# Moving two norms, their PSUM banks and two weight buffers in a two-block layer on one core

## The chip, the cores and the metric

The kernel runs on one core of one Trainium2 chip. The metric is device time in microseconds; before the change the median of three runs is 2661.46 us (2647.43 to 2663.86).

## The reference, cut to what matters

Two transformer blocks follow each other on 1024 tokens of 1024 features. What the change touches is the place where each mixer hands over to its feed-forward part, and the place where the first feed-forward hands over to a gate.

```python
# first block
y = concat([rmsnorm(y_c, g_out_conv), rmsnorm(y_a, g_out_attn)])
x = x + y @ w_out
h = rmsnorm(x, g_ffn)
gate = causal_dwconv3(h @ w_gate, ffn_conv_w, ffn_conv_b)
x = x + (silu(gate) * (h @ w_up)) @ w_down          # D_FF = 2816
x = x + sigmoid(rmsnorm(x, g_ple) @ w_ple_gate) * (p @ w_ple_proj)
# second block
x = x + concat([out_a, out_b]) @ w_out_2
h2 = rmsnorm(x, norm2_w)
x = x + (silu(h2 @ w_gate_2) * (h2 @ w_up_2)) @ w_down_2
```

## The kernel before

Features lie on the partitions, tokens on the free axis, in tiles of 128 x 1024; the tokens are worked on in two halves of 512. A product of full precision is three matmuls (lines 99 to 101): weights and activations are split into a high and a low part (the copy of line 93 on ScalarE, the subtraction of line 94 on VectorE or GpSimd) and high x high, high x low, low x high are added up in one PSUM bank.

A norm (class `Norm`) gathers squares of each tile into `acc` (line 129 on ScalarE, line 130 on VectorE). `rstd` then needs two banks, which it takes from the ring that it is given: four matmuls with ones (line 142) put the sums into the first, VectorE scales them (line 108), GpSimd raises them to the power -1/2 (line 109), and four transposes (line 145) spread the result over the second bank, from which VectorE reads it while it scales the tiles (line 157 in `apply`, line 645 in `Operands`).

The up and gate products of the feed-forward (`Quads`) use seven products per 2 x 2 group of weight and token halves, named 1, 2, 6, 7, 5, 4, 3. The first four pairs of weight tiles (gate and up in turn) go together: products 1 and 2 of all four need only the first half of the tokens (`Operands.first`), so eight products are issued before the first that needs the second half (`Operands.second`: norm of the second half, eight scalings at line 645, twelve subtractions at lines 669 to 672, four splits, and the loads of each pair's other weight tile at line 712, into buffers that the scalings set free). Each product is twelve matmuls. The eight products use all eight banks, two a pair. Weights pass through a ring of eight split buffers. Products 1 and 2 are taken out of the banks at line 804 (ScalarE) and line 806 (VectorE).

`out_part` multiplies the normed attention with its half of `w_out`, eight groups of twelve matmuls for a half of the tokens, adds to the residual at line 616, stores it (line 618 on SP's queue) and feeds the norm. Its banks come from `c.ring`, all eight in order.

`Down` runs the down product in four stages of eleven steps, with its own ring of split buffers that includes the `whi` and `wlo` tiles. The last three steps of stage 3 are held back and run bank by bank. `s4` holds six tiles of weight sums for stage 3. After it, `ple` loads the gate's weights (line 83) into the two `c.wraw` tiles in turn, splits them into `whi` and `wlo` tiles and multiplies.

Buffers of 128 x 1024 are units of one list: `take` pops the one that was given back longest ago, `take_last` the newest; an instruction that writes a taken unit waits for the last users of that unit. The order of the instructions on each engine is worked out when the kernel is built, with the program's order as priority, so neighbouring steps interleave; it is fixed from then on.

Of the kernel before, what the change touches and what calls it, by code (L numbers as in the profile page):

```python
# [20 lines left out]
HALF = (slice(0, 512), slice(512, 1024))  # L21
# [82 lines left out]
def rsqrt(c, ss, n, scale, eps):  # L104

    nc = c.nc
    r = c.small.tile([128, 32], F32, name="rq")
    nc.vector.tensor_scalar(r[:, 0:n], ss, scale, eps, OP.mult, OP.add)  # L108
    nc.gpsimd.tensor_tensor(r[:, 16:16 + n], r[:, 0:n], c.mhalf[:, 0:n], OP.pow)  # L109
    return r[:, 16:16 + n]  # L110


class Norm:
# [20 lines left out]
    def rstd(self, hs, ring):  # L134

        c = self.c
        nc = c.nc
        p, b = ring(), ring()
        n = 4 * len(hs)
        for j in range(n):  # L140
            o = hs[j // 4] * 512 + j % 4 * 128
            nc.tensor.matmul(p[:, j:j + 1], self.acc[:, o:o + 128], c.ones, start=True, stop=True)
        r = rsqrt(c, p[:, 0:n], n, 1.0 / self.nfeat, self.eps)
        for j in range(n):
            nc.tensor.transpose((b, p)[j // 4][:, j % 4 * 128:j % 4 * 128 + 128],
                                r[:, j:j + 1].to_broadcast([128, 128]), c.ident)
        return (b, p)[:len(hs)]

    def last(self, ring):
        rb, = self.rstd((1,), ring)  # L150
        self.c.give(self.acc)
        return rb
# [17 lines left out]
def pairs(his, los):  # L170
    return [(a.bitcast(F32R), b.bitcast(F32R)) for a, b in zip(his, los)]
# [343 lines left out]
def mixer1(c, a, h, xs, proj, norm_x):  # L515

    acts = pairs(*h)
    ring = Cycle(c.bank[0:2])
    tabs = c.takes(2)
    c.tab = Cycle(tabs)  # L520
    c.q, c.k, c.v, c.ya = {}, {}, {}, {}
    c.yc = [c.dr.tile([128, 1024], F32, name=f"yc{j}") for j in range(4)]

    def fill():
        yield from first
        norm_c = Norm(c, 512, c.vec["g_out_conv"], 1e-6)
        cv = conv_branch(c, a, acts, ring, norm_c)
        g1 = qkv_group(c, a, 1, acts, ring)
        for g, n in ((cv, 12), (g1, 24), (cv, 12)):
            for _ in range(n):  # L530
                next(g)
                yield
        next(cv, None)
        c.give(*h)
        yield from out_conv(c, a, ring, xs, norm_c, at)
        while len(c.ya) < 4:
            yield
        ya.extend(c.ya[i] for i in range(4))
        hi.extend(c.takes(4))
        lo.extend(c.takes(4))  # L540
        at.norm.apply(ya, hi, lo, 0, ring)
        yield
        yield from out_part(c, a["w_out"][1], pairs(hi, lo), ring, xs, (0,), norm, ws=ws, store=c.xf)
        rb.extend(norm.rstd((0,), ring))

    norm, ws = Norm(c, D, c.vec["g_ffn"], 1e-6), {}
    ya, hi, lo, rb = [], [], [], []
    first = qkv_group(c, a, 0, acts, ring)
    for i in range(17):
        next(first)  # L550
        if i in (1, 3):
            next(norm_x)
        if i >= 1:
            next(proj, None)
    filler = fill()
    at = Attention1(c, a, ring)
    for _ in at.pack(0):
        next(filler)
    at.run(filler, (2.08, 2.2, 2.5, 2.68))
    c.give(tabs)  # L560
    for _ in filler:
        pass
    ops = Operands(c, 4)
    at.norm.apply(ya, hi, lo, 1, Cycle(c.bank[2:4]))
    c.give(ya)
    ops.first(norm, xs, rb[0])
    quads = Quads(c, ops, hidden_pairs(a["w_gate"], a["w_up"]))
    for _ in out_part(c, a["w_out"][1], pairs(hi, lo), c.ring, xs, (1,), norm, ws=ws, store=c.xf):
        pass
    c.give(hi, lo)  # L570
    return quads, norm.last


def out_conv(c, a, ring, xs, n, at):

    nc = c.nc
    hi, lo = [], []
    rb = n.rstd((0, 1), ring)
    c.give(n.acc)
    for j in range(4):  # L580
        yc, p, l = c.takes(3)
        hi.append(p)
        lo.append(l)
        nc.sync.dma_start(yc, c.yc[j])
        for h in range(2):
            n.one(yc, j, p, l, h, rb[h], nc.gpsimd if h else nc.vector)
        c.give(yc)
        if j % 2:
            yield
    at.sums()  # L590
    yield from out_part(c, a["w_out"][0], pairs(hi, lo), ring, xs, (0, 1), load=a["xT"])
    c.give(hi, lo)
# [97 lines left out]
class Quads:  # L690
# [42 lines left out]
    def run(self, jobs, rstd, last):  # L733

        c, g = self.c, self.GROUP
        self.prep(2 * g)
        late, banks = {2 * g + 1: 7, 3 * g: 5, 3 * g + 2: 4, 3 * g + 4: 3}, {}
        for i, (n, p) in enumerate(self.steps):  # L740
            if i == 2 * g:
                self.acts.second(rstd(Cycle([banks[0][1], banks[1][1]])),
                                 lambda j: self.load(j, 1, c.take_last()))
            if i >= 2 * g:
                self.prep(i + 8)
            if i in late:
                self.acts.rest(late[i])
            if n not in banks:
                banks[n] = c.ring(), c.ring()
            bank = banks[n][0 if p in (1, 6, 5, 3) else 1]  # L750
            self.product(p, bank, self.ops.pop(0))
            if n == len(jobs) - 1:
                c.give(self.acts.u.pop(p))
                last(p, self)
            jobs[n](p, bank)
# [125 lines left out]
class Down:  # L881
# [53 lines left out]
    def operands(self, stage, j):  # L935
        c = self.c
        tt = c.nc.vector.tensor_tensor
        x, v = self.x.pop((stage, j)), self.v.pop((stage, j), None)
        if stage == 0:
            return self.parts(self.kept[j]), self.parts(x)  # L940
        if stage == 1:
            if j % 2 == 0:
                self.s4.append(c.take())
            u, w = self.kept.pop(j), c.take()
            tt(w[:, LO], v[:, LO], v[:, HI], OP.add)
            tt(w[:, LO], w[:, LO], u[:, LO], OP.subtract)
            tt(w[:, HI], u[:, LO], v[:, LO], OP.subtract)
            tt(self.s4[j // 2][:, HALF[j % 2]], u[:, HI], w[:, LO], OP.subtract)
            r = self.parts(w), self.parts(x)
            c.give(w)  # L950
            if j < 4:
                self.xs[2 * j + 1] = self.dma(u, self.xd[2 * j + 1])
            else:
                c.give(u)
            return r
        if stage == 2:
            tt(v[:, LO], v[:, LO], v[:, HI], OP.add)
            return self.parts(v), self.parts(x)
        return self.parts(self.s4[j // 2][:, HALF[j % 2]]), self.parts(x)

    def product(self, j, i, m, p, ops):
        w, x = ops
# [24 lines left out]
    def run(self):  # L987
        c, n = self.c, self.N
        extra = self.ring.items[:4]
        for stage, ps in enumerate(STAGES):  # L990
            tail = []
            for j in range(n):
                at = stage * n + j
                self.load(at + 6)
                ops = self.operands(stage, j)
                if stage == 3 and j >= n - 3:
                    tail.append((j, ops))
                    continue
                for i, p in enumerate(ps):
                    for m in range(4):  # L1000
                        self.product(j, i, m, p, ops)
                if stage == 0 and j in (4, 5, 6, 7):
                    t = 2 * (j - 4)
                    self.xs[t] = c.take()
                    self.dma(self.xs[t][:, LO], self.xd[t][:, LO])
                elif stage == 2 and j in (4, 5, 6, 7):
                    t = 2 * (j - 4)
                    self.dma(self.xs[t][:, HI], self.xd[t][:, HI])
                elif stage == 3 and j == 3 and self.norm is not None:
                    xl = [self.xs[m] for m in range(8)]  # L1010
                    nh, nl = c.takes(8), c.takes(8)
                    self.norm.apply(xl, nh, nl, 0, Cycle(self.b))
            if stage < 3:
                self.sums(stage)
            else:
                for m in range(4):
                    for j, ops in tail:
                        self.product(j, 0, m, 3, ops)
                    self.add(2 * m, 1, self.a[m])
        c.give(extra, self.s4, self.ring_x.items)  # L1020
        c.wraw = c.takes(2)
        if self.norm is None:
            return None
        return xl, (nh, nl), lambda: self.norm.apply(xl, nh, nl, 1, Cycle(self.b))
# [875 lines left out]
```

## Time and profile before

| | |
|---|---|
| median of 3 runs | 2661.46 us (2647.43 to 2663.86) |
| the profiled execution, its own time | 2663.26 us |
| its span, first to last instruction | 2661.5 us |
| mean granted TensorE clock | 0.968 |
| PE, busy | 2549.1 us |
| VectorE / ScalarE / GpSimd, busy | 1722.6 / 1121.5 / 318.7 us |

Times in the rows are microseconds from the start of the span. A row of a timeline gives the start, the duration, the engine, the source line, the operation with its result and operands, how many were merged, and in brackets how long the engine had been idle before and whose work ended that. PE is matmul, DVE is VectorE, ACT is ScalarE, POOL is GpSimd, SPq is the queue on SP that issues the transfers. A clock of 1.00 is 2.4 GHz, one of 0.50 is 1.2 GHz. Work of line 142 and 145 is recorded with one or two records for each instruction.

### The profile page before, as it was taken

How to read it: one execution, taken by the hardware profiler on the slowest of the kernel's cores; microseconds unless marked ns; L12 is line 12 of the kernel's file. 1: busy time of each engine (PE TensorE's matmuls, PEld its weight loads, DVE VectorE, ACT ScalarE, POOL GpSimd, SP SyncE). 2: the span in 40 equal slices, each digit the busy share in tenths (PEclk: the TensorE clock that was granted, in tenths of full speed). 3: DMA queues.
4: the chain of work that ended last, by engine and by line, in shares of the span. 5: the costliest groups of instructions: out<-in, count | busy, mean ns of one | idle time of the engine just before them, and what ended most of it. 6: DMA issues, size and time to landing. Idle time of an engine off the chain costs nothing.

```text
span 2661.5 us, 35653 instructions
## 1 busy us (share of the span) xinstructions
PE 2549.1 (96%) x13706; PEld 2114.5 (79%) x13706; DVE 1722.6 (65%) x3020; ACT 1121.5 (42%) x1913; POOL 318.7 (12%) x299
## 2 busy tenths in 40 slices
PE   8999999977999999999899999989996999999999
PEld 7978877765888887888689989877775888888787
DVE  6443445446877776776666899695658665565854
ACT  5333434233544444334444656544554433333332
POOL 3101001020000000000342233352220000000000
PEclk9999999978999999999899999899997999999999
DMA  6111113011232325744352322331111332237643
GB/s 224 48 40 40 49 48 127 33 64 64 99 108 107 111 105 171 245 138 135 115 204 75 118 78 96 111 108 48 33 68 68 131 107 95 99 108 249 215 154 118
DMA packets 103322, 289.59 MB, mean 109 GB/s; under 512 B 11208, under 2 KB 20464, under 8 KB 103152
## 3 DMA queue, kind: packets, MB, share of 16 engines
q1 hardware_dynamic: 101360, 281.03, 30.9%
q0 software_dynamic: 1792, 6.29, 0.6%
q8 instruction: 107, 1.75, 0.3%
q14 instruction: 63, 0.52, 0.1%
HBM read 211.77 MB, written 75.51 MB: 108 GB/s over the span
## 4 chain that ended last, share of the span: by engine, by line
PE 81%; DVE 9%; DMA 3%; issue 3%; ACT 2%; POOL 1%; SPq 0%; POOLq 0%; DVEq 0%; ACTq 0%
PE m L99 19%; PE m L100 19%; PE m L101 19%; PE m L426 3%; PE m L276 3%; PE m L278 3%; PE m L277 3%; PE m L417 3%; DVE t L94 2%; PE m L398 2%; PE m L397 2%; DVE t L1173 1%; DMA t<-in_w_down_dram 1%; ACT t L93 1%; POOL t L94 1%
## 5 line engine op out<-in xcount | busy, mean ns | idle before, releaser
L99 PE MATMUL m<-t,t 128*128 128x512 f32 x2520 | 976.1, 398 | 61.9 <-ACT t L93 55.2
L100 PE MATMUL m<-t,t 128*128 128x512 f32 x2520 | 989.2, 393 | 2.9 <-DVE t L94 2.3
L101 PE MATMUL m<-t,t 128*128 128x512 f32 x2520 | 975.4, 393 | 1.1 <-DVE t L94 1.1
L93 ACT ACTIVATE t<-t 128x512 fp32r<-128x512 f32 (+1 forms) x706 | 520.4, 758 | 872.2 <-PE m L100 612.6
L94 DVE TENSOR_TENSOR t<-t,t 128x512 fp32r<-128x512 f32 (+1 forms) x650 | 571.3, 900 | 274.0 <-ACT t L93 260.0
L99 PEld LDWEIGHTS m<-t,t 128*128 128x128 f32 x2520 | 480.0, 191 | 172.9 <-ACT t L93 61.0
L100 PEld LDWEIGHTS m<-t,t 128*128 128x128 f32 x2520 | 478.0, 190 | 103.7 <-DVE t L94 4.1
L101 PEld LDWEIGHTS m<-t,t 128*128 128x128 f32 x2520 | 476.7, 189 | 103.9 <-DVE t L94 3.5
L276 PE MATMUL m<-t,t 128*128 128x256 f32 x896 | 263.2, 294 | 3.1 <-DVE t L1613 2.5
L278 PE MATMUL m<-t,t 128*128 128x256 f32 x896 | 258.5, 289 | 3.5 <-DVE t L94 2.8
L277 PE MATMUL m<-t,t 128*128 128x256 f32 x896 | 257.6, 288 | 0.0
L109 POOL TENSOR_TENSOR rq<-rq,mhalf 128x4 f32<-128x4 f32 (+1 forms) x56 | 80.1, 1432 | 1005.7 <-DVE rq L108 988.5
L276 PEld LDWEIGHTS m<-t,t 128*128 128x128 f32 x896 | 174.9, 195 | 9.2 <-DVE t L1613 3.1
L278 PEld LDWEIGHTS m<-t,t 128*128 128x128 f32 x896 | 174.9, 195 | 5.9 <-DVE t L94 3.2
L277 PEld LDWEIGHTS m<-t,t 128*128 128x128 f32 x896 | 175.0, 195 | 1.9 <-issue 1.4
L403 ACT ACTIVATE t<-t,ar 128x256 f32<-128x256 f32 (+7 forms) x128 | 98.9, 773 | 92.3 <-DVE ar L400 89.2
L426 PE MATMUL m<-t,t 128*64 128x128 f32 x1152 | 107.5, 290 | 1.3 <-ACT t L423 0.7
L1170 ACT ACTIVATE t<-t,yss 128x896 f32<-128x896 f32 (+2 forms) x96 | 86.1, 897 | 47.1 <-DVE yss L1183 37.4
L423 ACT ACTIVATE t<-m 128x512 f32<-128x512 f32 (+3 forms) x128 | 56.6, 461 | 108.4 <-PE m L417 108.1
L616 DVE TENSOR_TENSOR t<-m,t 128x512 f32<-128x512 f32 x72 | 49.3, 688 | 79.6 <-PE m L101 75.7
L426 PEld LDWEIGHTS m<-t,t 128*64 128x64 f32 x1152 | 74.9, 141 | 32.0 <-issue 22.3
L400 DVE CUSTOM_DVE_ANT_0 t<-m,t 128x512 f32<-128x512 f32 (+3 forms) x128 | 73.8, 586 | 40.9 <-PE m L398 16.0
(225 smaller groups left out, 2649.2 us busy)
## 6 DMA issues: line engine op xcount, KB each, us to landing
t<-hd SPq DMA_DIRECT2D x66, 512.0 KB, 3.6
t<-in_w_down_dram SPq DMA_DIRECT2D x66, 512.0 KB, 4.3
t<-in_w_gate_dram SPq DMA_DIRECT2D x48, 512.0 KB, 3.8
t<-in_w_up_dram SPq DMA_DIRECT2D x44, 512.0 KB, 3.7
hd<-t SPq DMA_DIRECT2D x44, 512.0 KB, 2.9
hd<-t SPq DMA_DIRECT2D x66, 256.0 KB, 2.5
t<-in_w_out_dram SPq DMA_DIRECT2D x16, 512.0 KB, 3.5
xf<-t SPq DMA_DIRECT2D x32, 256.0 KB, 2.0
```

The source lines that it names most:

```text
L93: self.nc.scalar.activation(hi.bitcast(F32R), x, AF.Copy)
L94: (eng or self.nc.vector).tensor_tensor(lo.bitcast(F32R), x, hi, OP.subtract)
L99: nc.tensor.matmul(out, w[0], a[0], start=first, stop=False, skip_group_check=skip)
L100: nc.tensor.matmul(out, w[0], a[1], start=False, stop=False, skip_group_check=skip)
L101: nc.tensor.matmul(out, w[1], a[0], start=False, stop=last, skip_group_check=skip)
L109: nc.gpsimd.tensor_tensor(r[:, 16:16 + n], r[:, 0:n], c.mhalf[:, 0:n], OP.pow)
L276: nc.tensor.matmul(out, ah, wk[0], start=k == 0, stop=False)
L277: nc.tensor.matmul(out, ah, wk[1], start=False, stop=False)
L278: nc.tensor.matmul(out, al, wk[0], start=False, stop=k == NK - 1)
L403: nc.scalar.activation(p[:, :n], p[:, :n], AF.Exp, bias=least, scale=-1.0, accum_out=c.den[:, j:j + 1])
L426: nc.tensor.matmul(o[r], self.v(2 * hp + e, kb), ps[e][:, kb * 128:(kb + 1) * 128], start=kb == 0, stop=kb == qi)
L1170: nc.scalar.activation(ja[:, :s.shape[1]], s, AF.Sign, bias=NV[:, j:j + 1], accum_out=ca[:, j:j + 1])
```

## The change

Three places are edited.

1. In the first block, the norm of the feed-forward's first half no longer gets its `rstd` at the end of the work that fills the attention, in banks 0 and 1. It gets it after the second half of the attention's own norm, and both use banks 2 and 3, in the same order.
2. In `Quads.run` (both blocks), `second` is issued after the first pair's two products instead of after all eight, and its `rstd` uses the two banks of the fourth pair instead of one each of the first and second. The banks of the four pairs are handed out ahead, in the order as before.
3. In `Down`, each `s4` tile is given back as soon as it has been split in stage 3, and with a norm to follow (first block) the two `wraw` tiles are taken in step 3 of stage 3, ahead of the sixteen tiles of the normed result, instead of at the end.

```diff
@@ mixer1
         at.norm.apply(ya, hi, lo, 0, ring)
         yield
         yield from out_part(c, a["w_out"][1], pairs(hi, lo), ring, xs, (0,), norm, ws=ws, store=c.xf)
-        rb.extend(norm.rstd((0,), ring))
...
     ops = Operands(c, 4)
-    at.norm.apply(ya, hi, lo, 1, Cycle(c.bank[2:4]))
+    two = Cycle(c.bank[2:4])
+    at.norm.apply(ya, hi, lo, 1, two)
     c.give(ya)
-    ops.first(norm, xs, rb[0])
+    ops.first(norm, xs, norm.rstd((0,), two)[0])
@@ Quads.run
         self.prep(2 * g)
         late, banks = {2 * g + 1: 7, 3 * g: 5, 3 * g + 2: 4, 3 * g + 4: 3}, {}
+        for n in range(g):
+            banks[n] = c.ring(), c.ring()
         for i, (n, p) in enumerate(self.steps):
-            if i == 2 * g:
-                self.acts.second(rstd(Cycle([banks[0][1], banks[1][1]])),
-                                 lambda j: self.load(j, 1, c.take_last()))
+            if i == 2:
+                self.acts.second(rstd(Cycle(banks[g - 1])), lambda j: self.load(j, 1, c.take_last()))
@@ Down.operands
-        return self.parts(self.s4[j // 2][:, HALF[j % 2]]), self.parts(x)
+        r = self.parts(self.s4[j // 2][:, HALF[j % 2]]), self.parts(x)
+        if j % 2 or j == self.N - 1:
+            c.give(self.s4[j // 2])
+        return r
@@ Down.run
                 elif stage == 3 and j == 3 and self.norm is not None:
+                    c.wraw = c.takes(2)
                     xl = [self.xs[m] for m in range(8)]
                     nh, nl = c.takes(8), c.takes(8)
...
-        c.give(extra, self.s4, self.ring_x.items)
-        c.wraw = c.takes(2)
+        c.give(extra, self.ring_x.items)
```

## Rows read from the trace of the kernel before

**Rows 1.** The page, section 1: busy us (share of span) x instructions

```profile
PE 2549.1 (96%) x13706; PEld 2114.5 (79%) x13706; DVE 1722.6 (65%) x3020; ACT 1121.5 (42%) x1913; POOL 318.7 (12%) x299
```

**Rows 2.** The waits of PE, whole span: waiter, releaser, us, times, longest

```profile
PE m L99 <- ACT t L93: 55.2, 10, 14.5
```

**Rows 3.** PE's timeline after the first attention: start, us, engine, line, count, idle before

```profile
578.45 1.71 PE L142 MATMUL m<-ones,t 128*128 128x1 f32 x8
...
589.89 1.11 PE L145 MATMUL m<-ident,rq 128*128 128x128 f32 x4 [9.73 <-POOL rq L109]
...
592.50 3.78 PE L99 MATMUL m<-t,t 128*128 128x512 f32 x8 [1.50 <-ACT t L93]
```

**Rows 4.** DVE's timeline there

```profile
577.15 0.69 DVE L130 TENSOR_TENSOR t<-t,t 128x512 f32<-128x512 f32 x1 [0.63 <-ACT t L129]
...
578.70 5.36 DVE L645 SCALAR_TENSOR_TENSOR t<-t,vecs,m 128x512 f32<-128x512 f32 x8 [0.86 <-PE m L145]
```

**Rows 5.** POOL's timeline there

```profile
580.25 8.62 POOL L94 TENSOR_TENSOR t<-t,t 128x512 fp32r<-128x512 f32 x7 [2.58 <-PE m L142]
...
588.83 1.00 POOL L109 TENSOR_TENSOR rq<-rq,mhalf 128x4 f32<-128x4 f32 x1
```

**Rows 6.** PE's timeline, first block, from eighth product to full rate

```profile
638.95 0.94 PE L142 MATMUL m<-ones,t 128*128 128x1 f32 x8
...
656.42 1.40 PE L99 MATMUL m<-t,t 128*128 128x512 f32 x2 [14.54 <-ACT t L93]
...
664.79 0.80 PE L101 MATMUL m<-t,t 128*128 128x512 f32 x1 [0.52 <-DVE t L94]
...
670.56 0.39 PE L99 MATMUL m<-t,t 128*128 128x512 f32 x1
```

**Rows 7.** DVE's timeline, first block, from end of sums to second norm

```profile
619.02 1.48 DVE L130 TENSOR_TENSOR t<-t,t 128x512 f32<-128x512 f32 x2
...
622.89 0.69 DVE L806 TENSOR_TENSOR t<-m,t 128x512 f32<-128x512 f32 x1 [2.39 <-PE m L101]
...
641.92 5.36 DVE L645 SCALAR_TENSOR_TENSOR t<-t,vecs,m 128x512 f32<-128x512 f32 x8 [1.83 <-PE m L145]
```

**Rows 8.** SP's queue there, first of four loads

```profile
643.40 0.33 SPq L712 DMA_DIRECT2D t<-in_w_gate_dram  x1
```

**Rows 9.** Windows, first block: us, busy by engine, granted clock, DMA

```profile
650.00:665.00 15.00, 4.59 (x8) 2.08 (x9) 15.00 (x26) 8.98 (x15) 0.00 (x0) 0.50 0.06 24
```

**Rows 10.** DVE's timeline, second block

```profile
1993.39 1.46 DVE L94 TENSOR_TENSOR t<-t,t 128x512 fp32r<-128x512 f32 x1
...
2005.97 3.79 DVE L130 TENSOR_TENSOR t<-t,t 128x512 f32<-128x512 f32 x5
...
2021.93 5.36 DVE L645 SCALAR_TENSOR_TENSOR t<-t,vecs,m 128x512 f32<-128x512 f32 x8 [1.61 <-PE m L145]
```

**Rows 11.** PE's timeline, end of first down product and start of gate

```profile
1264.13 0.95 PE L142 MATMUL m<-ones,t 128*128 128x1 f32 x8
...
1270.74 0.60 PE L145 MATMUL m<-ident,rq 128*128 128x128 f32 x4
...
1282.11 0.39 PE L101 MATMUL m<-t,t 128*128 128x512 f32 x1
...
1293.64 0.79 PE L99 MATMUL m<-t,t 128*128 128x512 f32 x1 [11.14 <-ACT t L93]
...
1298.06 0.44 PE L99 MATMUL m<-t,t 128*128 128x512 f32 x1
```

**Rows 12.** The waits of SP's queue there

```profile
SPq L83 <- DVE t L130: 8.8, 2, 8.3
```

**Rows 13.** ACT's timeline there

```profile
1288.01 0.63 ACT L129 ACTIVATE t<-t 128x512 f32<-128x512 f32 x1 [0.21 <-DVE t L130]
...
1292.54 1.06 ACT L93 ACTIVATE t<-t 128x1024 fp32r<-128x1024 f32 x1 [3.89 <-DMA t<-in_w_ple_gate_dram]
```

**Rows 14.** POOL's timeline, second block

```profile
1986.75 10.95 POOL L94 TENSOR_TENSOR t<-t,t 128x512 fp32r<-128x512 f32 x8 [1.30 <-ACT t L93]
```

More of the change, by code (lines that the diff above doesn't have):

```diff
@@ L543, in fill @@
         yield from out_part(c, a["w_out"][1], pairs(hi, lo), ring, xs, (0,), norm, ws=ws, store=c.xf)
-        rb.extend(norm.rstd((0,), ring))
     norm, ws = Norm(c, D, c.vec["g_ffn"], 1e-6), {}
-    ya, hi, lo, rb = [], [], [], []
+    ya, hi, lo = [], [], []
     first = qkv_group(c, a, 0, acts, ring)
```

## The prediction

> **What bounds the kernel now.** I read the page first: PE is busy for 96% of the span [rows 1], so only stretches in which PE waits, or runs slowly, can be won. Next the waits of PE: one kind stands out, the first matmul of a product waiting for ScalarE's split, 55.2 us in ten waits [rows 2]. PE's timeline shows where the long ones lie, and each is a place that the change edits.
>
> Place A, after the first attention. PE's in-order queue holds the transposes of the attention's second-half norm (line 145), and they start only at 589.89, after 9.73 us of waiting for the power on GpSimd [rows 3]. The sums they need were complete at 577.84, when VectorE ended line 130; but VectorE then did eight scalings of the other norm (578.70 to 584.06) [rows 4], and GpSimd did seven splits for them, 580.25 to 588.87, before it reached the power at 588.83 [rows 5]. The norm that PE needs stands behind work that PE needs 25 us later. The output product starts at 592.50.
>
> Place B, in both feed-forwards. PE ends the eighth product at 638.95, makes the sums of the second norm, and then starts product 6 at 656.42 after 14.54 us of idling; its third matmul kind comes at 664.79 and full rate at 670.56 [rows 6]. VectorE is what runs meanwhile: its scalings start at 641.92 [rows 7], the first of the four loads for these weights is issued at 643.40 [rows 8], and from 650 to 665 VectorE is busy 15.00 of 15.00 us with PE's clock granted at 0.50, the 1.2 GHz level, after that idling [rows 9]. The second block repeats it, with the scalings at 2021.93 [rows 10].
>
> Place C, the ple gate. PE ends the down product at 1282.5 and waits 11.14 us, until 1293.64 [rows 11]. The waits of SP's queue say why: line 83, the load of the gate's weights, waited up to 8.3 us for VectorE's line 130 [rows 12]. The two `wraw` units were the only free ones left, and the norm's last squares had used them.
>
> **Rates.** Product 2 is evacuated at 622.89 [rows 7] and product 8 ends at 638.95 [rows 6]: six products in 16.1 us, 2.68 us each or 0.223 us a matmul. So product 1 began near 617.5.
>
> **Part A.** One `rstd` moves behind the other: the same four sums, one scaling, one power, four transposes, no instruction added or removed. In before's rows the chain is 1.71 us for the sums at the slow clock and 2.61 us from the transposes' start to the first matmul [rows 3]; the power takes 1.00 us [rows 5], and some 0.6 us go for VectorE's step and hand-overs (my estimate, from the gaps of these rows). That is 5.9 us after 577.84, 583.8 instead of 592.50: 8.7 us won, 7 if PE also makes the other norm's sums first (1.7 us). I take 8.6. What is late next: the moved norm must wait for the four readers of bank 3, then its eight scalings (5.4 us), ScalarE and eight GpSimd splits, 1.23 us each, run beside the output product. Scalings from about 587 to 592 and splits until 600 end well before product 1, now at 608.9; that cover is about 8 us. `out_part`'s fourth group wants bank 3 as well, at about 594, 2 us behind the last scaling; if the transposes are issued 6 us late, PE loses up to 6 us there. VectorE has, beside it, the residual additions it had before.
>
> Here a rule of the chip speaks against the move. In the second block eight GpSimd splits already run beside the output product, 1986.75 to 1997.70 [rows 14], and VectorE's split took 1.46 us there [rows 10], where an operation of that shape alone takes 0.69 [rows 7]. In the first block five of VectorE's splits and accumulations would now lie beside them: 5 x 0.7 = 3.5 us, and the sums before place B, complete 2.2 us before product 2 ends [rows 7], would be at most 1.3 us late. The Trainium skill ("SBUF — State Buffer", section "SBUF: two separate sides") says that VectorE with two SBUF inputs and GpSimd lock the shared port pair for a whole instruction and the loser fully blocks. By that rule the five could each lose a whole GpSimd split of 1.23 us, 6 us in all, the sums would be about 4 us late and the forecast some 3 us higher; the row shows about half of that for one instruction.
>
> **Part B.** `second` is moved past six products: one `rstd`, eight scalings, twelve subtractions, four splits (24 on VectorE, about 0.6 us apart), four on ScalarE, and four loads on SP. The loads pass nothing that waits long: SP then holds only the residual's stores, whose additions end before. The earliest it can start is the later of the sums' end and product 2's end. Product 2 then ends at 608.9 + 5.4 = 614.3. From sums to scalings took 2.97 us in before (638.95 to 641.92) [rows 6, 7], when PE had nothing else to do. Where PE has, the build's order puts products between: 1264.13 to 1270.74, 6.6 us [rows 11], the shortest of three such pairs; then 0.7 us to the scalings. Between 617.3 and 621.6 I take 620.6, near the late end since the three pairs resemble the new place.
>
> From there VectorE's chain sets product 6, in before and after alike. In before PE did 21 matmuls (4.7 us) from 638.95 to full rate at 670.56, so its steady run began in effect at 665.9, 24.0 us after the scalings. The same chain after 620.6, and two or three evacuations of line 806 that fall into it (1.5 us), gives 646.1. Won in the first block, A and B together: 665.9 - 646.1 = 19.8 us, of which B is 11.2. Ends: 23.1 (transposes at once) plus 2.6 if the clock does not fall, and 13 with the losses named under A. The bank costs nothing: the fourth pair's second product comes at about 629, the scalings have left its bank by 626.
>
> In the second block the sums are late: VectorE runs five accumulations of line 130 in a row from 2005.97, ending at 2009.76 [rows 10], while product 2 ends near 2002.9 (2.97 us and six products before 2021.93). So PE's queue may meet the sums a few us early and stall; that is hidden, as PE would idle before product 6 anyway. Scalings then start between 2012.7 and 2017.1, against 2021.93; less 1.8 us of evacuations inside the chain this wins 7.4 to 3.1 us. I take 5.
>
> **Part C.** Two oldest units instead of the last two: nothing wrote them since stage 1 or so, so the loads can go when SP has issued the inputs of stage 3; ScalarE waited 3.89 us for one that it had nothing else to do beside [rows 13], so one issued by 1278 costs nothing. The early return of `s4` makes up for the two units, and costs nothing itself. What is late next is the split buffer: `whi` and `wlo` are used by the last held-back steps, so ScalarE's split (1.06 us [rows 13]) can start only at PE's end, 1282.5, and PE at 1284.0 if ScalarE is free. If the build puts the norm's squares first, which end at 1288.64 [rows 13], PE starts at 1289.7. In before the loss was 13.6 us: full rate came at 1298.06 after nine matmuls (2.0 us) [rows 11]. In after it is 1.5 to 3 us, or at the other end 9.2 with 2 us of slow clock. Won: 12 to 4.4; I take 9, nearer to the early end, since the split needs only PE's end, the squares also an addition after it.
>
> **The sum.** 19.8 + 5 + 9 = 33.8 us off the profiled execution's own 2663.26 gives 2629.5; that execution lies 1.8 us above the median, so 2661.46 - 33.8 = 2627.7, say 2628. A measurement of this kernel can tell about 1%, 26.6 us, from no change: the line is at 2634.9.
>
> **Rivals.**
> - The chains move little. Sums and transposes are placed late, GpSimd's splits slow VectorE, bank 3 holds the fourth group, and the gate's split stands behind the squares. For it: the 6.6 us pair and the 1.46 us split. Against it: none touches A's 8.7 us. 13 + 3 + 4 = 20 us, 2641. Chance 0.2. The change not doing what it says belongs here: the loads come early, but the split buffer holds the gate.
> - The chains move fully: transposes at once, PE's idling too short for the clock to fall. 25.7 + 10 + 12 = 47.7, 2614. For it: PE idles 3 us instead of 14.5 before product 6. Against it: in A the same eight records of line 142 took 1.71 us at 578.45 and 0.94 at 638.95 [rows 3, 6], so a few us of sparse work had brought the clock down. Chance 0.15.
> - Slower: PE's in-order queue meets the second norm's sums before VectorE has made them. The place is line 142 between products 2 and 3; each us that the seven accumulations of line 130 are late holds PE, then `second`, by one. The second block's five late ones show the mechanism at some 4 us. It decides once the sums are late by 34 us in both blocks together. If the accumulations fell behind the whole dense chain of 23 us in each block, it is 46 lost against 34 won: 2673. Against it: they precede that chain in the program. Chance 0.05.
>
> **How the numbers follow.** The forecast has 0.6, 2616 to 2642 by its terms' ends. Leaving one in ten out on each side, the range is 2606 to 2648. Faster by over 1%: 0.8 of the forecast's 0.6, all of the second rival and a tenth of the first, 0.65; slower by over 1% needs more than the last rival's 12 us, 0.03; within 1%, 0.32.
>
> **What would show it.** A: line 145's wait of 9.73 gone, and line 99 about 6 us after the attention's last line 130. B: line 645 some 3 to 7 us after product 2, line 142 between products 2 and 3, product 6 about 14.5 us after line 645, VectorE still dense then. C: line 83 before the down product ends, no wait for line 130, PE's gap near 1.5 us. Wrong it would be if PE waits longer at line 142 or for bank 3 than it gains, or if a new wait for a unit appears.

## The result, and the profile after

The changed kernel takes 2622.36 us in the median of four runs (2617.09 to 2630.38), beside 2655.07 us for the kernel before on the same chip: a ratio of 0.9878, 95% interval 0.9830 to 0.9927, that is 32.4 us less (19 to 45). A second set of runs of the same two kernels gave 0.9873, 0.9852 to 0.9894. Forecast were 2628 us, counted from a before of 2661.46, and 33.8 us off. The profiled execution took 2630.38 us itself.

Line numbers up to 712 are those of before; what was line 806 is now 807. First the page (span, and PE's busy time), then the waits of PE over the whole span (engine, line, releaser: total, times, longest), which answer to [rows 1] and [rows 2].

```profile
span 2628.6 us, 35665 instructions
...
PE 2546.4 (97%) x13706; PEld 2113.9 (80%) x13706; DVE 1721.3 (65%) x3020; ACT 1120.4 (43%) x1913; POOL 319.1 (12%) x299
```

```profile
PE m L99 <- ACT t L93: 28.5, 11, 7.9
PE m L99 <- DVE t L645: 5.5, 1, 5.5
...
PE m L142 <- DVE t L130: 3.4, 2, 2.8
```

The large kind of wait, ScalarE's split before a product's first matmul, went from 55.2 to 28.5 us; a new one, line 99 for VectorE's line 645, is 5.5 us long. PE's timeline after, at the four places (start, duration, engine, line, operation, and in brackets the idle time before it and what ended it); it answers to [rows 3, 6, 11]:

```profile
575.09 1.14 PE L436 MATMUL m<-ident,rd 128*64 128x128 f32 x15
579.03 1.85 PE L142 MATMUL m<-ones,t 128*128 128x1 f32 x8 [2.80 <-DVE t L130]
581.13 1.87 PE L142 MATMUL m<-ones,t 128*128 128x1 f32 x8 [0.25 <-DVE rq L108]
582.85 1.09 PE L145 MATMUL m<-ident,rq 128*128 128x128 f32 x4
585.45 3.36 PE L99 MATMUL m<-t,t 128*128 128x512 f32 x7 [1.50 <-ACT t L93]
...
617.34 0.94 PE L142 MATMUL m<-ones,t 128*128 128x1 f32 x8
623.96 0.60 PE L145 MATMUL m<-ident,rq 128*128 128x128 f32 x4
640.89 1.40 PE L99 MATMUL m<-t,t 128*128 128x512 f32 x2 [7.87 <-ACT t L93]
...
1268.37 0.50 PE L99 MATMUL m<-t,t 128*128 128x512 f32 x1 [1.21 <-ACT t L93]
1270.43 0.50 PE L99 MATMUL m<-t,t 128*128 128x512 f32 x1 [1.33 <-ACT t L93]
...
1985.18 0.95 PE L142 MATMUL m<-ones,t 128*128 128x1 f32 x8
...
1989.64 0.60 PE L145 MATMUL m<-ident,rq 128*128 128x128 f32 x4
1995.69 0.80 PE L99 MATMUL m<-t,t 128*128 128x512 f32 x1 [5.45 <-DVE t L645]
2004.78 1.40 PE L99 MATMUL m<-t,t 128*128 128x512 f32 x2 [4.55 <-ACT t L93]
```

Place A: the 9.73 us before line 145 are gone; both norms' sums stand one behind the other, and the output product begins 6.5 us after the last addition (579.0). Place B: the sums stand about eight matmuls into product 3, without a wait, and the idle time before product 6 is 7.87 us instead of 14.54. Place C: two waits of 1.2 and 1.3 us instead of one of 11.14. In the second block PE now waits 5.45 us for a bank that the scalings hold, and then 4.55 for product 6.

VectorE's timeline, which answers to [rows 4, 7, 10], GpSimd's and ScalarE's at the same places:

```profile
594.87 0.68 DVE L616 TENSOR_TENSOR t<-m,t 128x512 f32<-128x512 f32 x1
...
599.01 2.89 DVE L130 TENSOR_TENSOR t<-t,t 128x512 f32<-128x512 f32 x2
601.83 1.78 DVE L94 TENSOR_TENSOR t<-t,t 128x512 fp32r<-128x512 f32 x1
603.53 0.68 DVE L616 TENSOR_TENSOR t<-m,t 128x512 f32<-128x512 f32 x1
...
611.52 1.48 DVE L130 TENSOR_TENSOR t<-t,t 128x512 f32<-128x512 f32 x2
615.69 0.69 DVE L807 TENSOR_TENSOR t<-m,t 128x512 f32<-128x512 f32 x1 [2.69 <-PE m L101]
...
624.60 5.36 DVE L645 SCALAR_TENSOR_TENSOR t<-t,vecs,m 128x512 f32<-128x512 f32 x8 [2.14 <-PE m L145]
...
1990.28 5.36 DVE L645 SCALAR_TENSOR_TENSOR t<-t,vecs,m 128x512 f32<-128x512 f32 x8 [3.54 <-PE m L145]
```

```profile
591.15 11.90 POOL L94 TENSOR_TENSOR t<-t,t 128x512 fp32r<-128x512 f32 x8 [2.06 <-ACT t L93]
...
618.56 1.01 POOL L109 TENSOR_TENSOR rq<-rq,mhalf 128x4 f32<-128x4 f32 x1 [15.51 <-DVE rq L108]
```

```profile
1267.26 1.06 ACT L93 ACTIVATE t<-t 128x1024 fp32r<-128x1024 f32 x1 [0.22 <-PE m L101]
```

The second norm's sums are complete at 613.0, before product 2 is evacuated at 615.69. The power is done at 619.57, but PE's order brings the transposes at 623.96, so the scalings begin at 624.60. The gate's first split begins when PE has ended the down product, as the prediction had it. The windows (busy time of PE, PE's loads, VectorE, ScalarE, GpSimd, then the granted clock, DMA share and GB/s) answer to [rows 9]: VectorE is still dense, and PE's clock still goes to 0.50, the 1.2 GHz level, after the idling, while at the gate it now stays at 1.00.

```profile
635.00:640.00 5.00, 0.00 (x0) 0.00 (x0) 5.00 (x9) 2.83 (x5) 0.00 (x0) 0.71 0.00 2
640.00:645.00 5.00, 3.10 (x5) 1.36 (x5) 5.00 (x10) 3.10 (x5) 0.00 (x0) 0.50 0.00 0
...
1267.00:1272.00 5.00, 2.46 (x10) 1.61 (x10) 5.00 (x8) 3.77 (x7) 1.27 (x1) 1.00 0.24 92
```

**Where the time went, place by place.** A single part is worth less than the times alone can tell, so I paired the n-th matmul record of PE in each run with the n-th of before, and read how much the distance changes across each place: A between the records at 574.8 and 601.3 us of before, B between 624.0 and 673.1, C between 1282.1 and 1321.7, the gate's own stage between 1346.7 and 1358.9, B in the second block between 2011.9 and 2052.1. The gate's own stage follows place C and is not edited. "Else" is the rest between PE's first and last matmul, no part of it edited.

| run | A | B first | C | gate stage | B second | else |
|---|---|---|---|---|---|---|
| after, first profile | -8.7 | -8.7 | -11.5 | +0.9 | -4.2 | -1.6 |
| again (the same kernel) | -8.7 | -9.8 | -11.3 | +0.8 | -2.8 | -11.8 |
| a_only | -10.1 | -0.5 | -1.3 | 0.0 | -0.3 | -6.1 |
| b_only | -0.8 | -9.8 | -1.4 | 0.0 | -3.4 | -9.4 |
| c_only | 0.0 | -0.1 | -10.2 | 0.0 | -0.1 | +2.5 |
| s4_only | -0.1 | -0.1 | -13.5 | +7.5 | -0.3 | -0.2 |
| i4 | -8.7 | -6.7 | -11.6 | +0.8 | -3.1 | -15.9 |
| put6 | -8.7 | -6.9 | -11.3 | +0.8 | -0.5 | -12.0 |
| late | -10.1 | -8.7 | -13.5 | +7.4 | -3.8 | -7.3 |
| late_n | -8.7 | -10.1 | -13.5 | +6.4 | -1.8 | -11.9 |
| swap | -8.7 | -10.0 | -11.5 | +0.9 | -3.4 | -10.5 |
| first_v | -8.8 | -7.5 | -11.4 | +0.8 | -4.4 | -10.1 |

The changed kernel gains 32 us at the edited places in each of its two profiles, near the 32.4 and 33.7 of the times; what "else" adds is variation between executions, most of it from one stretch in which the profiled execution of before ran at the lower clock (last section).

### The profile page after: what moved, and what is told of

Its sections match the earlier page's. It is cut to its first block, busy times and chain, and to the rows that moved or that the text cites. A ratio compares the mean times of both kernels' runs of the same rounds, so it can differ in the third digit from the quotient of the medians.

```text
span 2628.6 us, 35665 instructions
## 1 busy us (share of the span) xinstructions
PE 2546.4 (97%) x13706; PEld 2113.9 (80%) x13706; DVE 1721.3 (65%) x3020; ACT 1120.4 (43%) x1913; POOL 319.1 (12%) x299
## 3 DMA queue, kind: packets, MB, share of 16 engines
q8 instruction: 107, 1.75, 0.3%
## 4 chain that ended last, share of the span: by engine, by line
PE 62%; issue 27%; DVE 7%; DMA 2%; ACT 2%; POOL 1%; SPq 0%; DVEq 0%; POOLq 0%; ACTq 0%
PE m L99 13%; PE m L100 12%; PE m L101 12%; PE m L426 3%; PE m L276 3%; PE m L278 3%; PE m L277 3%; PE m L417 3%; PE m L398 2%; PE m L397 2%; DVE t L94 1%; DVE t L1177 1%; PE m L1459 1%; DVE t L157 1%; PE m L1456 1%
## 5 line engine op out<-in xcount | busy, mean ns | idle before, releaser
L99 PE MATMUL m<-t,t 128*128 128x512 f32 x2520 | 975.1, 397 | 41.0 <-ACT t L93 28.5
L417 PE MATMUL m<-ident,t 128*128 128x128 f32 x576 | 96.1, 289 | 2.7 <-ACT t L1536 1.3
```

Source lines behind the costliest of these rows:

```text
L99: nc.tensor.matmul(out, w[0], a[0], start=first, stop=False, skip_group_check=skip)
L417: nc.tensor.transpose(tb[:, j * 128:(j + 1) * 128], ps[e][:, (g + j) * 128:(g + j + 1) * 128], c.ident)
```

## The experiments

**The parts one by one.** Each of the first three is the kernel before with one numbered part of the change, as the diff of the change has it; cut here to its main lines (`...` stands for the others).

```diff
a_only:  -        rb.extend(norm.rstd((0,), ring))
         ...
         -    ops.first(norm, xs, rb[0])
         +    ops.first(norm, xs, norm.rstd((0,), two)[0])
b_only:  -            if i == 2 * g:
         +            if i == 2:
         ...
c_only:  +        if j % 2 or j == self.N - 1:
         +            c.give(self.s4[j // 2])
         ...
         +                    c.wraw = c.takes(2)
         ...
         -        c.wraw = c.takes(2)
```

> The kernel before with the first edit alone: the power of the ffn norm's first half is asked for behind the sums of the attention's second-half norm. Theory: the matmul stream, matmul for matmul against the kernel before, comes 8 to 9 us earlier at the output product (place A) and carries this to the end of the first feed-forward, since the second-half norm, left where it was, waits for the eighth product and not for anything that the first edit delays. The end is 7 to 10 us earlier and nothing else moves. Rival: the eight GpSimd splits that now lie beside the output product slow VectorE's splits and accumulations so much that its sums come late, and 3 us or less of the gain are left at product 6. The whole is 0.3% or so, below what times alone can tell: the place of each step is read from the trace.

> The kernel before with the second edit alone: the second half's norm is asked for behind product 2 in both feed-forwards. Theory: the matmul stream gains about 8 us in the first block and about 4 in the second, and PE still idles about 8 us before product 6 of the first block, since the chain behind the scalings, not their start, then sets product 6. In the second block PE waits some 5 us for a bank that the scalings hold, in front of the fourth pair's second product; this wait lies ahead of an idle stretch and adds nothing. Rival 1, that the wait for the bank adds to the end: the second block gains nothing. Rival 2, that the whole way from product 2 to product 8 is won: 11 us or more in the first block, with under 3 us of idling before product 6.

> The kernel before with the third edit alone: the two units of the gate's weights are taken in the third stage of the feed-forward, and the units of the fourth stage's operands go back one by one. Theory: all of it shows at the ple gate in the first block, 9 to 11 us earlier from there on, with PE waiting under 2 us in front of the gate and its granted clock unbroken; nothing before and nothing behind moves. Rival: ScalarE's split, which needs the buffers of the last held-back steps, and not the load, was what PE waited for: then under 3 us.

Measured: a_only 0.9946 (0.9930 to 0.9963), b_only 0.9934 (0.9915 to 0.9953), c_only 0.9964 (0.9947 to 0.9981). By place: A gains 10.1 us alone, and B's idle time behind it stays 14.54 us, so nothing of it is swallowed there. B gains 9.8 and 3.4, with 7.89 us of idling left before product 6 and the bank's 5.45 us in the second block. C gains 10.2, with 2.5 us of waits at the gate and the clock at 0.74 in one window of 5 us, where I had expected under 2 and no break. The theories hold otherwise; the rivals by which place A keeps 3 us or less, the second block gains nothing or C gains under 3 us fall, and so does the one by which all of B's way is won. The sum by place, 33.5, is near that of the changed kernel's two profiles, 33.1 and 32.6 without the gate's stage. The three ratios alone would give some 14, 17.5 and 9.5 us, 41 together, by their intervals with about 8 us to either side: the times cannot tell whether the parts add up. C's place moved by 1.3 us in a_only and b_only too, where nothing of it is edited: so much is the uncertainty of one row of the table.

**Which half of C.** Before, with the early return alone (cut):

```diff
...
+        if j % 2 or j == self.N - 1:
+            c.give(self.s4[j // 2])
...
-        c.give(extra, self.s4, self.ring_x.items)
+        c.give(extra, self.ring_x.items)
         c.wraw = c.takes(2)
```

> The kernel before with half of the third edit: the units of the fourth stage's operands go back one by one, but the two units of the gate's weights are taken where they were, at the end. Theory: the wait was for units that the norm's squares had just used, so any two units that come free earlier would do; the last two of the fourth stage's operands come free a few us before the end of the down product, the loads go 15 us or so earlier than in the kernel before, and 5 to 10 us of the 10 at the gate are won. Rival: the units that are taken at the end are still those of the norm's squares, whatever came back before; then PE waits some 11 us as before, and the early taking is the whole of the third edit.

Measured 0.9988 (0.9974 to 1.0003). Three views of s4_only: the load's first issue (first and last start at the end of the row), PE's timeline, and windows.

```profile
L83 SPq DMA_DIRECT2D t<-in_w_ple_gate_dram x16: 327/332/333, 1259.3 to 1347.8; - x16
```

```profile
1282.73 0.50 PE L101 MATMUL m<-t,t 128*128 128x512 f32 x1 [1.01 <-DVE t L94]
...
1341.22 1.87 PE L142 MATMUL m<-ones,t 128*128 128x1 f32 x8 [4.13 <-DVE t L130]
```

```profile
1340.00:1345.00 5.00, 3.78 (x13) 3.39 (x14) 2.68 (x4) 2.34 (x4) 2.17 (x2) 0.60 0.74 221
1345.00:1350.00 5.00, 5.00 (x18) 3.93 (x17) 1.92 (x2) 1.95 (x4) 2.51 (x2) 0.71 0.60 210
```

The loads go at 1259.3, 29 us before those of before and 23 us before PE ends the down product, and that is enough: PE waits 1.01 us at the gate. With the units taken in the third stage, in the changed kernel, the first issue is at 1118.5, and the place gains 2 us less. So two units that the squares do not hold did as well, taken at either place, and the early taking is not the whole of the third edit. But 60 us later PE meets the sums of the gate's first-half norm before VectorE's last addition, waits 4.13 us and goes on at the lower clock, and 7.5 of the 13.5 us are given back. That loss I had not foreseen.

**The changed kernel with the units taken at the end.** late is the changed kernel with that taking; late_n also asks for the gate's first-half norm two products later in the program.

```diff
late:    -                    c.wraw = c.takes(2)
         +        c.wraw = c.takes(2)
late_n:  (late, and in the gate's loops)
         +            if (hh, m) == (1, 2):
         +                norm.apply(xs, *h, 0, c.ring)
         -        norm.apply(xs, *h, hh, c.ring)
         +    norm.apply(xs, *h, 1, c.ring)
```

> The changed kernel with the two units of the gate's weights taken at the end again, where they were before; the early return of the fourth stage's operands stays. Theory: as alone, so here: the gate starts with no wait for ScalarE's split, 2 to 3 us earlier than in the changed kernel, since the split is then made for a later moment and stands in another order; and the loss that followed in that run, PE waiting 4.1 us in front of the sums of the next norm and then running at the lower clock, comes back as well, 5 to 8 us: in all 3 to 5 us slower than the changed kernel. Rival: that loss belonged to the order of that build alone; then 2 to 3 us faster.

> The run with the gate's units taken at the end, and with it the norm of the gate stage's first half asked for behind the second product of the second half instead of before its first: the same place that the feed-forward's norm has. Theory: PE waited 4.1 us in front of those sums because they stood in its order before VectorE's last addition was done; standing some ten products' thirds later they find the addition done, the wait and the lower clock behind it go, 7 us, and the 2 us at the gate are kept: 2 us less than the changed kernel by the trace. Rival: GpSimd's multiplications of the gate, 1.8 us each, are what this stage is short of, and the wait comes back at the next step that needs it, with a gain under 2 us over the run before.

Measured: late 0.9889 (0.9862 to 0.9916), late_n 0.9898 (0.9882 to 0.9915), no better than the changed kernel. Both gain 13.5 us at the gate and lose 7.4 and 6.4 behind it. By place the theory of late holds, with 4.5 us less than the changed kernel for gate and gate stage together; that of late_n falls. PE's timeline of late, then of late_n, and GpSimd's of late_n:

```profile
1317.55 1.52 PE L142 MATMUL m<-ones,t 128*128 128x1 f32 x8 [3.97 <-DVE t L130]
```

```profile
1314.91 1.87 PE L142 MATMUL m<-ones,t 128*128 128x1 f32 x8 [2.61 <-DVE t L130]
```

```profile
1310.90 1.84 POOL L1052 TENSOR_TENSOR t<-t,t 128x512 f32<-128x512 f32 x1 [3.33 <-ACT t L1051]
```

In the built program the sums stand only six matmuls later in PE's order than in late, and the wait is shorter by what six matmuls take, 1.4 us; the addition still isn't done. The rival falls too as far as it says that GpSimd is short of time: it had been idle for 3.33 us before this multiplication. What the sums wait for is a chain of five steps, one behind the other: ScalarE's sigmoid (from 1310.24), this multiplication, the residual's addition, the square and the last addition, which ends at 1314.85, while PE ran out of other work at 1312.30. Whether an order with the sums some twelve matmuls later, 2.6 us, keeps both gains was not tried.

**Where in the order the second norm stands.** The changed kernel, with the norm asked for behind the fourth product, and with the fourth group's two banks exchanged:

```diff
i4:      -            if i == 2:
         +            if i == 4:
swap:    -                self.acts.second(rstd(Cycle(banks[g - 1])), lambda j: self.load(j, 1, c.take_last()))
         +                self.acts.second(rstd(Cycle(banks[g - 1][::-1])), lambda j: self.load(j, 1, c.take_last()))
```

> The changed kernel with the second half's norm asked for behind the fourth product instead of the second. In the built program the sums then stand 15 matmuls later in PE's order in the first block, and so do the transposes, 3.4 us. Theory: the way from the transposes to product 6 is VectorE's chain, and each us by which the transposes stand later is a us of PE's idling before product 6: +3 to +4 us in the first block. Rival: product 6 waits for something else, ScalarE's splits or the weights, and comes within 1 us of where it was.

> The changed kernel with the fourth group's two banks given to the norm in the other order: the sums in the second bank, the transposes in the first, which the scalings then hold. Theory: in the second block PE's wait for the bank, 5.45 us, moves to the group's other product or stays in its size, and product 6 starts where it did, within 1 us, since VectorE's and ScalarE's chain sets it and not the bank. Rival: the wait adds to the end, and product 6 and the end move by what the wait does, 2 to 3 us, one product's time.

PE's timeline of i4:

```profile
620.54 0.50 PE L99 MATMUL m<-t,t 128*128 128x512 f32 x1 [2.91 <-DVE t L645]
629.63 1.40 PE L99 MATMUL m<-t,t 128*128 128x512 f32 x2 [4.50 <-ACT t L93]
```

In i4 B's first place gains 6.7 us instead of 9.8 (the changed kernel again, of the same set of runs) or 8.7: sums and transposes stand 14 matmuls later in PE's order, 3.2 us in the trace, and that comes out as 2.0 to 3.1 us. The time of the whole, 0.9878 (0.9847 to 0.9908), can't tell that. In the second block the built order has both where the changed kernel has them, so nothing is tested there. In the first block i4 also shows a wait for the bank: 2.91 us of wait for it and 4.50 of idling before product 6, together 7.4 beside the 7.9 of the changed kernel; the loss shows in the shorter waits that follow in product 6, 5.2 us instead of 2.9.

In swap (0.9883, 0.9869 to 0.9898) the wait in the second block has the same 5.45 us, and the places gain 10.0 and 3.4: no answer to what the wait costs, since it did not change. The changed kernel's own trace answers it for the start of product 6 in the second block. VectorE's timeline there:

```profile
1995.55 1.89 DVE L669 TENSOR_TENSOR t<-t,t 128x512 f32<-128x512 f32 x3
...
2003.38 0.69 DVE L770 TENSOR_TENSOR t<-t,t 128x512 f32<-128x512 f32 x1
```

From the scalings' start, 1990.28, to line 770's end at 2004.07 VectorE has no gap, so it waits for nothing of PE's; ScalarE's split starts right behind, at 2004.10, and PE's product 6 behind that, at 2004.78. PE's wait for the bank lies beside this chain and not in it; without it PE would have idled longer before product 6. No run took it away.

**What lies beside VectorE's chain.** The changed kernel with product 6's four splits moved to GpSimd, and with the first half's eight moved from GpSimd to VectorE:

```diff
put6:    -            self.put(6, j, d[:, LO])
         +            self.put(6, j, d[:, LO], c.nc.gpsimd)
first_v: -                self.put(p, j, t[:, s], c.nc.gpsimd)
         +                self.put(p, j, t[:, s])
```

> The changed kernel with the four splits that product 6 needs of its activations moved from VectorE to GpSimd, which is idle there. Theory 1: VectorE's chain between the scalings and product 6 gets shorter by four splits of 0.6 us, PE idles 2 to 2.5 us less before product 6 in each block. Theory 2, by what the changed kernel showed beside the output product, where GpSimd's splits took 1.49 us instead of 1.23 and VectorE's 1.4 to 1.8 instead of 0.69: the two engines hold each other up, four splits cost VectorE about as much as they took, and GpSimd's own take 6 us in a row: product 6 comes 0 to 3 us later.

> The changed kernel with the eight splits of the first half's activations on VectorE instead of GpSimd, in both blocks: no GpSimd work beside VectorE's any more. Theory: in the first block there was room, the sums were done 2.7 us before the second product was evacuated, and VectorE's extra 8 times 0.6 us, less the 0.7 to 2.2 us that each of its operations beside GpSimd gets back, come to nothing at product 6, within 1 us. In the second block VectorE has no room: its five additions come up to 5 us later less the same return, and product 6 comes 0 to 4 us later. Rival, by the two engines holding each other up: without GpSimd VectorE does all of it sooner, and product 6 comes 2 us or more earlier in one of the blocks.

VectorE's timeline of put6, with one line of the changed kernel again (the last) to compare, then GpSimd's in the two blocks, then PE's:

```profile
628.29 0.68 DVE L807 TENSOR_TENSOR t<-m,t 128x512 f32<-128x512 f32 x1
628.89 1.16 DVE L769 TENSOR_TENSOR t<-t 128x512 f32<-128x512 f32 x1
629.97 1.75 DVE L770 TENSOR_TENSOR t<-t,t 128x512 f32<-128x512 f32 x1
631.64 1.75 DVE L773 TENSOR_TENSOR t<-t,t 128x512 f32<-128x512 f32 x1
...
629.23 0.68 DVE L770 TENSOR_TENSOR t<-t,t 128x512 f32<-128x512 f32 x1
```

```profile
625.56 7.28 POOL L94 TENSOR_TENSOR t<-t,t 128x512 fp32r<-128x512 f32 x3 [15.99 <-ACT t L93]
...
1992.45 14.99 POOL L94 TENSOR_TENSOR t<-t,t 128x512 fp32r<-128x512 f32 x4 [12.83 <-ACT t L93]
```

```profile
632.43 0.80 PE L99 MATMUL m<-t,t 128*128 128x512 f32 x1 [9.43 <-ACT t L93]
```

Theory 2 of put6 holds: three GpSimd splits take 7.28 us, 2.4 each beside the 1.23 of [rows 5], and PE waits 9.43 us before product 6 instead of 7.9. Most of VectorE's operations beside them keep their 0.68 us, but four take 1.16 to 1.75: they lose 3.7 us together, more than the 2.4 us that the four splits took on VectorE, 0.6 each. B gains 1.8 to 2.9 us less in the first block and 2.3 to 3.7 less in the second, where the four splits take 14.99 us and PE waits 5.1 us for one of them, so GpSimd itself is late there. The time of the whole, 0.9878 (0.9856 to 0.9899), doesn't show it. In first_v the first block loses 1.2 to 2.3 us against the changed kernel's two profiles (its additions end 1.3 us later, and so stand the sums; within 1 us was expected), the second block comes within what it varies (-4.4 beside -4.2 and -2.8): no loss is seen there, and not the rival's gain in either block. The expectation's 2.2 us for one operation is too much: the row at 599.01 above holds two, and the five slow ones beside GpSimd's splits lost 0.3 to 1.1 us each. Its whole, 0.9895 (0.9871 to 0.9919), tells no difference.

## Why the prediction was right, and where its sizes were off

**Bound.** Right: the edits moved only stretches in which PE waited or ran slowly, and the sum of the edited places is the time won.

**The sum.** In the first profile 17.4 us for A and B in the first block, 4.2 in the second and 11.5 at the gate, less 0.9 lost in the gate's own stage: 32.2 against 33.8. That it came so near is in part luck: the forecast was 2.4 us too high in the first block and 0.8 in the second, and 2.5 too low at the gate. The 2628 us were counted from a median of three runs, 2661.46; a fourth run made it 2655.07, and so the changed kernel's time lies 5.6 us under the forecast with a gain that is 1.4 us smaller.

**Part A, 8.6 us.** Measured 8.7 in most runs and 10.1 in two. I had 5.9 us from the last addition to the first matmul; it took 6.5. The clock had fallen by the time PE's 2.80 us of waiting for the addition were over (granted 0.54 from 579 to 580), and the eight records of either norm's sums took 1.85 us. PE did make the other norm's sums first, for which I had allowed 1.7 us; they fell into the way over VectorE and GpSimd, whose power was done at 582.23, and held the transposes back by 0.6 us. In a_only the same records took 1.05 and 1.19 us, and the way 5.1 us: there the granted clock was 1.00 until 573, behind the wait, so when the clock falls is not the same in each execution. What I had named as next, bank 3 and GpSimd's splits, cost PE nothing: the output product ran at full rate from 589, and the sums for place B were ready 2.7 us before product 2 was evacuated. The Trainium skill ("SBUF — State Buffer", section "SBUF: two separate sides") has the two engines lock a shared port pair for a whole instruction when VectorE reads two SBUF inputs; here the trace agrees in kind: beside GpSimd's eight splits, 1.49 us each, five operations of lines 94 and 130 took 0.95 to 1.78 us and lost 3.3 us together, near the 3.5 that I had from the rows, while line 616, which reads a bank, stayed at 0.68. VectorE made that up before the last additions, so neither the 1.3 us of lateness nor the 3 us that the rule would have added to the forecast came. (The 0.69 that I took from [rows 7] is of an operation that reads a bank; [rows 4] has the same 0.69 for line 130.)

**Part B, first block, 11.2 us.** Measured 8.7 to 10.1. The chain from the scalings to the steady run was right: in the first profile full rate came 16.2 us earlier than the 665.9 worked out for before, so in effect at 649.7, 25.1 us after the scalings, against the 25.5 forecast. The mis-sized term is "Between 617.3 and 621.6 I take 620.6": the scalings began 9.0 us after product 2, not 6.3. The pair of sums and transposes was 6.62 us apart, as in [rows 11], 1 us more than I took, and the sums themselves stood 1.8 us behind product 2 in PE's order, which I had put at nothing. The power was ready 4.4 us before the transposes came. That this is time lost is argued from i4, where sums and transposes 3.2 us later cost 2 to 3 us. An order with the transposes right behind the power was not tried.

**Part B, second block, 5 us.** Measured 1.8 to 4.4, 4.2 in the first profile. The scalings began at 1990.28, or 3.9 us earlier than before when set against the 27.7 us won until there; my range for them ended 0.9 us sooner. PE did not meet the sums too early. "The bank costs nothing" was said of the first block, where no wait for it appears; in the second it is the longest new wait, 5.45 us, and by the trace it lies beside VectorE's chain and adds nothing to product 6's start.

**Part C, 9 us.** Measured 10.2 to 11.6. The early end of the two was the right one: the split (1267.26) waited for PE's end and nothing else, and the clock did not fall, so 2.5 us of waits were left of a loss of 13.6. That the split needs PE's end depends on the order of the build: in s4_only, with the loads at 1259.3, it was made at 1276.35, before that end, and 2 us more were won there.

**The rivals.** Chains that move little: its 13 us for A and B in the first block and its 4 at the gate were passed; its 3 in the second block lies within the 1.8 to 4.4 measured. Chains that move fully: of its 25.7 us for A and B in the first block 17.4 and 18.5 were measured in the changed kernel, and PE still idled and slowed before product 6; its 12 at the gate nearly came. Slower: line 142 had no wait at place B. It had one elsewhere, 60 us behind the gate, of 0.6 us in the changed kernel and 2.6 to 4.1 in s4_only, late and late_n, where it did cost 6.4 to 7.5 us.

**The signs.** Two did not come: line 645 stood 9.0 us after product 2 and not 3 to 7, and product 6 started 16.3 us after line 645 and not 14.5, in part since two evacuations, 1.4 us, now stand in VectorE's chain, which the sum had counted and the sign had not.

## What to carry over

In an in-order queue, ask of each small step what stands before it and what needs it first: two norms exchanged in order were worth 9 us, a load that did not wait for just-used buffers 11. Moving a chain's start earlier wins only as much as the order of the build lets its links follow; here the sums stood 1.8 us and the transposes 4.4 us behind the moment at which they could have run, and the forecast of place B had left out the first and 1 us of the second. Work put on an idle engine is not free when it keeps a busy one waiting: four splits on GpSimd cost VectorE 3.7 us and saved it 2.4.

## What was not expected of the hardware

The same instructions, in a stretch that no edit touches, ran at either clock level from one execution to the next. Windows of the changed kernel in its two profiles, the first and again:

```profile
525.00:530.00 5.00, 5.00 (x21) 2.81 (x22) 0.88 (x4) 3.03 (x6) 0.87 (x1) 0.50 0.02 3
```

```profile
525.00:530.00 5.00, 5.00 (x39) 3.18 (x35) 2.20 (x4) 1.86 (x4) 0.00 (x0) 1.00 0.00 0
```

PE was busy 5.00 of 5.00 us in both, and in the two windows before, from 515 to 525, too; in the first the granted clock stayed at 0.50, the 1.2 GHz level, until about 545, and the second came out of this stretch 8 us earlier. Of the 13 profiled executions four had the lower clock for some 20 us here, that of the kernel before among them, three for 3 to 7 us, and six not at all. What makes the difference is open. It is as much as one part of the change, it is why single parts were read at their places, and it is most of what "else" gives in the table.
